# The w_down stage of a hybrid mLSTM and attention block: factor loads on another queue, another order of products, two PSUM banks as one tile

## The chip, the cores and the metric

The kernel runs on one core of a Trainium2 chip. The metric is device time in microseconds (us) of one execution; lower is better. The core's engines work side by side, each through its own list of instructions in order: TensorE (PE in the profile, its weight loads PEld), VectorE (DVE), ScalarE (ACT), GpSimd (POOL) and SyncE (SP). SP, POOL and ScalarE can also start DMA transfers, each from its own queue.

## The reference

One encoder block on x (512 tokens x 2048), all in float32: an RMS norm and input projection, four mLSTM heads and eight differential attention heads, an output projection, and a SwiGLU channel mixer. The change touches only the last product of the mixer:

```python
h2 = rmsnorm(x, norm2_g[l])
x = x + (jax.nn.silu(h2 @ w_gate[l]) * (h2 @ w_up[l])) @ w_down[l]
return rmsnorm(x, final_g)
```

w_down has 5632 rows and 2048 columns.

## The kernel before

Every matmul is done in three: both operands are split into a high part (a ScalarE copy to float32r, L98) and a low part (a VectorE subtraction, L99), and `three` (L157) adds high x high, high x low and low x high. So each operand that comes from memory costs one ScalarE and one VectorE instruction.

The first 4096 rows of w_down are multiplied by Strassen's scheme in Winograd's form, in the loop at L1069. It runs over eight units u: ci, one of four row blocks of 1024, and dg, one of two column halves of 1024. A unit is seven products, P1 to P7, in the order of `DOWN`. A product is 24 matmuls of 512 columns in two PSUM banks (`acc` and `aux`), in two halves h; each half multiplies variants of the activations (left) with one factor of the weights (right).

*Factors.* The generator `left_factors` makes them: per unit and half h, `load` (L885) brings five 512 KB blocks from w_ds on SP's queue: B11 and B22 plainly, T1 and T3 as a plain load and then an accumulating load of a second block on POOL's queue (L891), and B21 plainly. VectorE adds T1 to B22 for P6 (L913) and B21 to it for P4 (L915). `upto` says how many loads the source has asked for at each product. Blocks lie in two rings of seven slots, `raw` (h = 0) and `raw2` (h = 1); `raw2` is opened when the stage before has ended. A factor is split into `whi` and `wlo`, rings of three, and `factor` keeps two more ahead of the one in use, one product.

*Variants.* The activations were written by the stage before to DRAM (`actv`), in seven forms of 256 columns for each row block. `variant` (L946) loads one form in two transfers of 256 KB on SP's queue, into `ra`, a ring of two, and splits each half at once into two tiles of the ring `A`. Both units of a row block use the same seven variants. Those of block 0 are made in the last group of the stage before (four) and in unit 0 (three); those of block ci + 1 in the unit with dg = 1 of block ci, one ahead of each product.

After a product its two banks are copied to `M` by ScalarE (ci = 0, L1088) or added to it by VectorE (L1090), one instruction a bank. After the loop `combine` puts the seven products together, and the other 1536 rows follow in plain products; `last_weights` (L1166) loads and splits the last of their weights while they run.

The order of the instructions on each engine is not that of the source. The framework takes, for each engine, the ready instruction that comes first in the source, by its own model of times; it also sets all waits. On the chip each engine then keeps that order. A tile's slot in a ring is given to the next tile that asks for one once the last reader of the old tile is done.

Of the kernel before, what the change touches and what calls it, by code (L numbers as in the profile page):

```python
# [19 lines left out]
NSP = 4  # L20
# [10 lines left out]
def build(nc, tc, ctx, a, out):  # L31
# [8 lines left out]
    pc = pool("small", 2)  # L40
    pa = pool("pa", 32)
    pW = pool("pw", 3)
    pacc = pool("acc", 4, space=bass.MemoryType.PSUM)
    paux = pool("aux", 4, space=bass.MemoryType.PSUM)
    dram = pool("dr", 1, space=bass.MemoryType.DRAM)

    def stage(*pools):
# [18 lines left out]
        return pT.tile([128, 512], dt, tag="T", name=nm("T"))  # L66

    def tacc():
        return pacc.tile([128, 512], F32, tag="acc", name=nm("acc"))

    def taux():
        return paux.tile([128, 512], F32, tag="aux", name=nm("aux"))

    def tc_(n, p=128, name="c"):
        return cp.tile([p, n], F32, tag=nm("t" + name), name=nm(name))
# [13 lines left out]
    c = {}  # L89
# [752 lines left out]
    def tW(tag, dt=F32, bufs=3):  # L842
        return pW.tile([128, 1024], dt, tag=tag, name=nm(tag), bufs=bufs)

    DOWN = ["P1", "P3", "P6", "P5", "P7", "P4", "P2"]
    more = []

    def tR():
# [2 lines left out]
    def left_factors():  # L851
        def loads(w, g):
            r = []
            for q in range(4):
                t = tW("raw", bufs=7)
                nc.sync.dma_start(t, a[w][g, q])
                r.append(t)
            return r

        def parts(src):  # L860
            hi, lo = tW("whi", F32R), tW("wlo", F32R)
            split(hi, lo, src)
            return hi, lo

        todo = [(w, g) for g in range(NFB) for w in ("w_g", "w_u")]
        nxt = loads(*todo[0])
        for i in range(len(todo)):
            w11, w12, w21, w22 = nxt
            yield parts(w11)
            s1 = tW("raw", bufs=7)  # L870
            V.tensor_tensor(s1, w21, w22, ALU.add)
            V.tensor_tensor(w21, w11, w21, ALU.subtract)
            V.tensor_tensor(w11, s1, w11, ALU.subtract)
            yield parts(w11)
            yield parts(w21)
            yield parts(s1)
            if i + 1 < len(todo):
                nxt = loads(*todo[i + 1])
            yield parts(w12)
            yield parts(w22)  # L880
            V.tensor_tensor(w12, w12, w11, ALU.subtract)
            yield parts(w12)


        def load(u, h, i, ring):  # L885
            j, n, j2, n2 = ((0, 0, 0, 0), (1, 1, 1, 1), (0, 0, 0, 1), (1, 1, 0, 1), (1, 0, 1, 0))[i]
            ci, dg = divmod(u, 2)
            t = ring()
            nc.sync.dma_start(t, a["w_ds"][ci, dg, j, n, h])
            if (j, n) != (j2, n2):  # L890
                G.dma_start(t, a["w_ds"][ci, dg, j2, n2, h], accum_op=ALU.add)  # L891
            return t

        order = [(u, i, h) for u in range(2 * NSP) for i in range(5) for h in range(2)]
        got = {}
        pos = [0]

        def upto(k):
            while pos[0] < min(k, len(order)):
                u, i, h = order[pos[0]]  # L900
                got[u, i, h] = load(u, h, i, tR if h and (u, i) != (0, 0) else lambda: tW("raw", bufs=7))
                pos[0] += 1

        upto(2)
        for u in range(2 * NSP):
            k = 10 * u
            for pi, name in enumerate(DOWN):
                if u or pi:
                    upto(k + (14 if pi == 0 else 16 if pi < 6 else 20))
                for h in range(2):  # L910
                    B11, B22, T1, T3, B21 = (got.get((u, i, h)) for i in range(5))
                    if name == "P6":
                        V.tensor_tensor(B22, B22, T1, ALU.add)  # L913
                    if name == "P4":
                        V.tensor_tensor(B22, B22, B21, ALU.add)  # L915
                    yield parts({"P1": B11, "P3": B22, "P6": B22, "P5": T1, "P7": T3, "P4": B22, "P2": B21}[name])
# [26 lines left out]

    cur_v = {}

    def variant(ci, name, into):  # L946

        v = ["P1", "P7", "P2", "P4", "P5", "P6", "P3"].index(name)
        into[name] = []
        for h in range(2):  # L950
            if more:
                r = more[2].tile([128, 512], F32, tag="ra", name=nm("ra"), bufs=2)
            else:
                r = tW("raw", bufs=7)[:, 0:512]
            g0 = 4 * ci + 2 * h
            nc.sync.dma_start(r.rearrange("p (g c) -> p g c", g=2), actv[g0:g0 + 2, v].rearrange("g p c -> p g c"))
            hi, lo = tA(), tA()
            split(hi, lo, r)
            into[name].append((hi, lo))

    def group(scale, done, first=False, last=False):

        banks = {}
        ps, u, C1, C2 = (tX() for _ in range(4))

        def bank(name):
            if name not in banks:
                banks[name] = (tacc, taux)[len(banks) % 2]()[:, L]
            return banks[name]

        def add(out_, name, other):
            V.tensor_tensor(out_, banks[name], other, ALU.add)

        def after(name):
            if name == "P1":
                SC.copy(ps[:, L], banks[name])
            if name == "P6":
                add(u[:, L], name, ps[:, L])
            if name == "P7":
                add(u[:, R], name, u[:, L])  # L980
            if name == "P5":
                add(C2[:, R], name, u[:, R])
                add(ps[:, R], name, u[:, L])
            if name == "P2":
                add(C1[:, L], name, ps[:, L])
            if name == "P4":
                add(C2[:, L], name, u[:, R])
                done(1, C2)
            if name == "P3":
                add(C1[:, R], name, ps[:, R])  # L990
                done(0, C1)

        order = list(ORDER)
        if first:
            xs = tXS()
            ws = {}
            for i, name in enumerate(order[:3]):
                ws[name] = factor(0)
                product(bank(name), ws[name], name_of(name), range(6))
                if i < 2:  # L1000
                    for j in (2 * i, 2 * i + 1):
                        h2_turn(3, xs, x1, j)
                    for _ in h2_sums(3, xs, slice(i, i + 1)):
                        pass
            for name in order[:3]:
                product(bank(name), ws[name], name_of(name), range(6, 8))
                after(name)
            order = order[3:]
            next(st2)
        for name in order:  # L1010
            w = factor()
            product(bank(name), w, name_of(name))
            if first and name == "P2":
                next(st2)
            after(name)
            if last:
                i = {"P1": 0, "P6": 1, "P5": 2, "P4": 3}.get(name)
                if i is not None:
                    variant(0, DOWN[i], cur_v)

    def name_of(p):
        return RIGHT[p]
# [34 lines left out]
    more.extend(stage(("rr", 1), ("ra", 1)))  # L1057
    more[1:] = more[1]
    M = [{}, {}]

    def product_down(banks, w, name, h):
        for m in range(2):
# [5 lines left out]

    for u in range(2 * NSP):  # L1069
        ci, dg = divmod(u, 2)  # L1070
        got_v = cur_v
        if dg == 1:
            cur_v = {}
        for pi, name in enumerate(DOWN):
            if u == 0 and pi < 3:
                variant(0, DOWN[4 + pi], cur_v)
            if dg == 1 and ci + 1 < NSP:
                variant(ci + 1, name, cur_v)
            banks = [tacc(), taux()]
            for h in range(2):  # L1080
                product_down(banks, factor(), name, h)
            if ci == 0:
                M[dg][name] = pM.tile([128, 1024], F32, tag="M", name=nm("M"), bufs=14)
            t = M[dg][name]
            for tt in range(2):
                cs = slice(tt * 512, tt * 512 + 512)
                if ci == 0:
                    SC.copy(t[:, cs], banks[tt])  # L1088
                else:
                    V.tensor_tensor(t[:, cs], banks[tt], t[:, cs], ALU.add)  # L1090

    more[0].close()
    limit[0] = len(seq)
    last, (pB,) = stage(("fb", 1),)
# [71 lines left out]
    def last_weights():  # L1166

        for b in range(CHUNKS[-1]):
            for n in range(4):
                r = tW("raw", bufs=7)  # L1170
                nc.sync.dma_start(r, a["w_d"][NFB - CHUNKS[-1] + b, n])
                for j in range(2):
                    hi, lo = tL(), tL()
                    split(hi, lo, r[:, j * 512:j * 512 + 512])
                    wL[n][0].append(hi)
                    wL[n][1].append(lo)
                yield

    for ci, nb in enumerate(CHUNKS[:-1]):
        q = chunks[ci]  # L1180
# [55 lines left out]
            nc.sync.dma_start(out[ts, n * 512:n * 512 + 512], xt[n])  # L1236
    last.close()
    mst.close()


def _layout(np, inp):
# [85 lines left out]
```

## Time and profile before

| | |
|---|---|
| time, median of 3 runs | 2180.97 us (2178.7 to 2186.47) |
| profiled execution, its own time | 2190.05 us |
| its span, first to last instruction | 2188.3 us |
| busy | TensorE 2142.0 us (98%), VectorE 1569.6 (72%), ScalarE 992.7 (45%), GpSimd 133.8 (6%) |
| mean granted TensorE clock | 0.991 |
| DMA, whole span | 292.56 MB, mean 134 GB/s |
| the w_down stage, units 0 to 7 | 1693.24 to 2043.60 us |

The profile is of one execution. Times of a row are us from the start of the span; a row's line (L98) is a line of the kernel before. "Idle before, releaser" is the time in which the engine had nothing to do ahead of an instruction, and what ended it. The granted clock is a share of TensorE's full speed; it has two levels, 1.00 (2.4 GHz) and 0.50 (1.2 GHz), and a stretch shows their mean.

### The profile page before, as it was taken

How to read it: one execution, taken by the hardware profiler on the slowest of the kernel's cores; microseconds unless marked ns; L12 is line 12 of the kernel's file. 1: busy time of each engine (PE TensorE's matmuls, PEld its weight loads, DVE VectorE, ACT ScalarE, POOL GpSimd, SP SyncE). 2: the span in 40 equal slices, each digit the busy share in tenths (PEclk: the TensorE clock that was granted, in tenths of full speed). 3: DMA queues.
4: the chain of work that ended last, by engine and by line, in shares of the span. 5: the costliest groups of instructions: out<-in, count | busy, mean ns of one | idle time of the engine just before them, and what ended most of it. 6: DMA issues, size and time to landing. Idle time of an engine off the chain costs nothing.

```text
span 2188.3 us, 33437 instructions
## 1 busy us (share of the span) xinstructions
PE 2142.0 (98%) x13305; PEld 1938.2 (89%) x13305; DVE 1569.6 (72%) x2362; ACT 992.7 (45%) x1515; POOL 133.8 (6%) x189
## 2 busy tenths in 40 slices
PE   9999999999999999999999999999999799999998
PEld 7888889988888889999999999999999577778786
DVE  6267776366544468888888888888889467779745
ACT  6256675355434354344344443343444454444423
POOL 0011110000000000000000000000000000001100
PEclk9999999999999999999999999999999999999999
DMA  6232112332234424343443434433335986876732
GB/s 257 96 96 78 62 53 72 116 97 87 82 112 146 140 92 131 124 145 119 129 135 119 137 121 133 131 123 117 121 121 168 284 228 184 242 210 156 203 106 77
DMA packets 100749, 292.56 MB, mean 134 GB/s; under 512 B 10976, under 2 KB 27376, under 8 KB 100592
## 3 DMA queue, kind: packets, MB, share of 16 engines
q1 hardware_dynamic: 86832, 247.42, 34.5%
q0 software_dynamic: 13760, 43.00, 8.4%
q8 instruction: 104, 1.70, 0.3%
q14 instruction: 53, 0.43, 0.1%
HBM read 264.16 MB, written 26.22 MB: 133 GB/s over the span
## 4 chain that ended last, share of the span: by engine, by line
PE 85%; DMA 6%; DVE 6%; ACT 2%; issue 1%; ACTq 0%; POOL 0%; DVEq 0%; SPq 0%; POOLq 0%
PE acc L159 9%; PE acc L158 9%; PE acc L160 9%; PE acc L933 8%; PE acc L932 8%; PE acc L931 8%; PE aux L933 6%; PE aux L932 6%; PE aux L931 6%; DMA ra<-actv 4%; PE acc L189 4%; PE acc L190 4%; PE acc L191 4%; DVE wlo L99 2%; PE aux L160 1%
## 5 line engine op out<-in xcount | busy, mean ns | idle before, releaser
L98 ACT CAST whi<-raw 128x1024 fp32r<-128x1024 f32 (+2 forms) x573 | 593.6, 1037 | 807.4 <-PE acc L932 238.8
L99 DVE TENSOR_TENSOR wlo<-raw,whi 128x1024 fp32r<-128x1024 f32 (+2 forms) x573 | 690.5, 1206 | 305.8 <-ACT whi L98 295.0
L158 PE MATMUL acc<-whi,A 128*128 128x512 f32 (+1 forms) x1056 | 404.0, 384 | 21.4 <-ACT whi L98 18.2
L159 PE MATMUL acc<-wlo,A 128*128 128x512 f32 (+1 forms) x1056 | 403.7, 382 | 9.5 <-DVE wlo L99 9.5
L160 PE MATMUL acc<-whi,A 128*128 128x512 f32 (+1 forms) x1056 | 400.7, 379 | 0.0
L158 PEld LDWEIGHTS acc<-whi,A 128*128 128x128 f32 x1056 | 200.0, 190 | 59.4 <-ACT whi L98 22.5
L159 PEld LDWEIGHTS acc<-wlo,A 128*128 128x128 f32 x1056 | 200.3, 190 | 48.0 <-DVE wlo L99 15.0
L160 PEld LDWEIGHTS acc<-whi,A 128*128 128x128 f32 x1056 | 200.4, 190 | 34.0
L932 PE MATMUL acc<-A,whi 128*128 128x256 f32 x704 | 199.3, 283 | 0.5 <-DVE A L99 0.5
L931 PE MATMUL acc<-A,whi 128*128 128x256 f32 x704 | 199.4, 283 | 0.0
L931 PE MATMUL acc<-h,whi 128*128 128x256 f32 x704 | 199.4, 283 | 0.0
L933 PE MATMUL acc<-h,wlo 128*128 128x256 f32 x704 | 199.2, 283 | 0.0
L932 PE MATMUL acc<-h,whi 128*128 128x256 f32 x704 | 199.2, 283 | 0.0
L933 PE MATMUL acc<-A,wlo 128*128 128x256 f32 x704 | 199.2, 283 | 0.0
L933 PE MATMUL aux<-h,wlo 128*128 128x256 f32 x528 | 149.7, 284 | 0.8 <-DVE wlo L99 0.8
L931 PE MATMUL aux<-h,whi 128*128 128x256 f32 x528 | 149.6, 283 | 0.6 <-ACT whi L98 0.6
L189 PE MATMUL acc<-A,whi 128*128 128x512 f32 x384 | 150.1, 391 | 0.0
L190 PE MATMUL acc<-A,whi 128*128 128x512 f32 x384 | 149.8, 390 | 0.0
L191 PE MATMUL acc<-A,wlo 128*128 128x512 f32 x384 | 149.8, 390 | 0.0
L933 PE MATMUL aux<-A,wlo 128*128 128x256 f32 x528 | 149.4, 283 | 0.0
L931 PE MATMUL aux<-A,whi 128*128 128x256 f32 x528 | 149.4, 283 | 0.0
L932 PE MATMUL aux<-A,whi 128*128 128x256 f32 x528 | 149.4, 283 | 0.0
(280 smaller groups left out, 4123.9 us busy)
## 6 DMA issues: line engine op xcount, KB each, us to landing
raw<-in_w_g_dram SPq DMA_DIRECT2D x88, 512.0 KB, 3.5
raw<-in_w_u_dram SPq DMA_DIRECT2D x88, 512.0 KB, 3.6
raw<-in_w_ds_dram SPq DMA_DIRECT2D x80, 512.0 KB, 5.1
raw<-in_w_aqk_dram SPq DMA_DIRECT2D x32, 512.0 KB, 3.4
raw<-in_w_o_dram SPq DMA_DIRECT2D x32, 512.0 KB, 3.5
raw<-in_w_ds_dram POOLq DMA_DIRECT2D x32, 512.0 KB, 8.2
raw<-in_w_b_dram SPq DMA_DIRECT2D x31, 512.0 KB, 4.0
actv<-x POOLq DMA_DIRECT2D x48, 256.0 KB, 3.4
```

Source lines behind the costliest of these rows:

```text
L98: SC.copy(hi, src)
L99: V.tensor_tensor(lo, src, hi.bitcast(F32), ALU.subtract)
L158: PE.matmul(acc, lh, rh, start=first, stop=False)
L159: PE.matmul(acc, lh, rl, start=False, stop=False)
L160: PE.matmul(acc, ll, rh, start=False, stop=last)
L189: PE.matmul(banks[f], wh[:, cs], xh[k], start=first, stop=False)
L190: PE.matmul(banks[f], wh[:, cs], xl[k], start=False, stop=False)
L191: PE.matmul(banks[f], wl[:, cs], xh[k], start=False, stop=last)
L931: PE.matmul(bank, w[0][:, cs], hi, start=m == 0, stop=False)
L932: PE.matmul(bank, w[0][:, cs], lo, start=False, stop=False)
L933: PE.matmul(bank, w[1][:, cs], hi, start=False, stop=m == 7)
```

## The change

- The order of the products is P1, P3, P2, P6, P5, P7, P4 (P2 was last), and the blocks of a unit are loaded in the order B11, B22, B21, T1, T3. The last step of `upto` (20 blocks ahead at the last product) is gone; it stays at 16.
- `variant` is divided: `load_v` starts the two transfers, now from ScalarE's queue, and `variant` later splits what was loaded first. In the source the load stands a product before the split. The first variant of block ci + 1 is loaded at product 4 and split at product 6 of the unit with dg = 0; the one used at P1 thus stands a unit before its use, and the others follow from product 1 on in the unit with dg = 1.
- A product's two banks are one PSUM tile of 128x1024, and one instruction copies or adds both. For that the eight single banks are closed before the stage and opened again after it.
- In `last_weights` the step ends between the load and its splits, so that the splits are asked for a step after their load.

```diff
--- before.py
+++ after.py
@@ -40,8 +40,15 @@
     pc = pool("small", 2)
     pa = pool("pa", 32)
     pW = pool("pw", 3)
-    pacc = pool("acc", 4, space=bass.MemoryType.PSUM)
-    paux = pool("aux", 4, space=bass.MemoryType.PSUM)
+    PS = bass.MemoryType.PSUM
+    banks8 = []
+
+    def open_banks():
+        st = ExitStack()
+        banks8[:] = [st] + [st.enter_context(tc.tile_pool(name=n, bufs=4, space=PS, reuse_waits="tile"))
+                            for n in ("acc", "aux")]
+
+    open_banks()
     dram = pool("dr", 1, space=bass.MemoryType.DRAM)
 
     def stage(*pools):
@@ -66,10 +73,10 @@
         return pT.tile([128, 512], dt, tag="T", name=nm("T"))
 
     def tacc():
-        return pacc.tile([128, 512], F32, tag="acc", name=nm("acc"))
+        return banks8[1].tile([128, 512], F32, tag="acc", name=nm("acc"))
 
     def taux():
-        return paux.tile([128, 512], F32, tag="aux", name=nm("aux"))
+        return banks8[2].tile([128, 512], F32, tag="aux", name=nm("aux"))
 
     def tc_(n, p=128, name="c"):
         return cp.tile([p, n], F32, tag=nm("t" + name), name=nm(name))
@@ -842,7 +849,7 @@
     def tW(tag, dt=F32, bufs=3):
         return pW.tile([128, 1024], dt, tag=tag, name=nm(tag), bufs=bufs)
 
-    DOWN = ["P1", "P3", "P6", "P5", "P7", "P4", "P2"]
+    DOWN = ["P1", "P3", "P2", "P6", "P5", "P7", "P4"]
     more = []
 
     def tR():
@@ -883,7 +890,7 @@
 
 
         def load(u, h, i, ring):
-            j, n, j2, n2 = ((0, 0, 0, 0), (1, 1, 1, 1), (0, 0, 0, 1), (1, 1, 0, 1), (1, 0, 1, 0))[i]
+            j, n, j2, n2 = ((0, 0, 0, 0), (1, 1, 1, 1), (1, 0, 1, 0), (0, 0, 0, 1), (1, 1, 0, 1))[i]
             ci, dg = divmod(u, 2)
             t = ring()
             nc.sync.dma_start(t, a["w_ds"][ci, dg, j, n, h])
@@ -906,9 +913,9 @@
             k = 10 * u
             for pi, name in enumerate(DOWN):
                 if u or pi:
-                    upto(k + (14 if pi == 0 else 16 if pi < 6 else 20))
+                    upto(k + (14 if pi == 0 else 16))
                 for h in range(2):
-                    B11, B22, T1, T3, B21 = (got.get((u, i, h)) for i in range(5))
+                    B11, B22, B21, T1, T3 = (got.get((u, i, h)) for i in range(5))
                     if name == "P6":
                         V.tensor_tensor(B22, B22, T1, ALU.add)
                     if name == "P4":
@@ -943,20 +950,26 @@
 
     cur_v = {}
 
-    def variant(ci, name, into):
-
+    loaded = []
+
+    def load_v(ci, name):
         v = ["P1", "P7", "P2", "P4", "P5", "P6", "P3"].index(name)
-        into[name] = []
         for h in range(2):
             if more:
                 r = more[2].tile([128, 512], F32, tag="ra", name=nm("ra"), bufs=2)
             else:
                 r = tW("raw", bufs=7)[:, 0:512]
             g0 = 4 * ci + 2 * h
-            nc.sync.dma_start(r.rearrange("p (g c) -> p g c", g=2), actv[g0:g0 + 2, v].rearrange("g p c -> p g c"))
+            SC.dma_start(r.rearrange("p (g c) -> p g c", g=2), actv[g0:g0 + 2, v].rearrange("g p c -> p g c"))
+            loaded.append((name, r))
+
+    def variant(into):
+
+        for h in range(2):
+            name, r = loaded.pop(0)
             hi, lo = tA(), tA()
             split(hi, lo, r)
-            into[name].append((hi, lo))
+            into.setdefault(name, []).append((hi, lo))
 
     def group(scale, done, first=False, last=False):
 
@@ -1016,7 +1029,9 @@
             if last:
                 i = {"P1": 0, "P6": 1, "P5": 2, "P4": 3}.get(name)
                 if i is not None:
-                    variant(0, DOWN[i], cur_v)
+                    if i:
+                        variant(cur_v)
+                    load_v(0, DOWN[i])
 
     def name_of(p):
         return RIGHT[p]
@@ -1057,6 +1072,9 @@
     more.extend(stage(("rr", 1), ("ra", 1)))
     more[1:] = more[1]
     M = [{}, {}]
+    banks8[0].close()
+    pst = ExitStack()
+    pairs = pst.enter_context(tc.tile_pool(name="pair", bufs=4, space=PS, reuse_waits="tile"))
 
     def product_down(banks, w, name, h):
         for m in range(2):
@@ -1068,27 +1086,37 @@
 
     for u in range(2 * NSP):
         ci, dg = divmod(u, 2)
-        got_v = cur_v
-        if dg == 1:
-            cur_v = {}
+        got_v = cur_v if ci == 0 else nxt_v if dg == 0 else got_v
         for pi, name in enumerate(DOWN):
-            if u == 0 and pi < 3:
-                variant(0, DOWN[4 + pi], cur_v)
-            if dg == 1 and ci + 1 < NSP:
-                variant(ci + 1, name, cur_v)
-            banks = [tacc(), taux()]
+            if u == 0 and pi < 4:
+                variant(cur_v)
+                if pi < 3:
+                    load_v(0, DOWN[4 + pi])
+            if ci + 1 < NSP:
+                if (dg, pi) == (0, 4):
+                    load_v(ci + 1, DOWN[0])
+                if (dg, pi) == (0, 6):
+                    nxt_v = {}
+                    variant(nxt_v)
+                    load_v(ci + 1, DOWN[1])
+                if dg == 1 and pi > 0:
+                    variant(nxt_v)
+                    if pi < 6:
+                        load_v(ci + 1, DOWN[pi + 1])
+            bank = pairs.tile([128, 1024], F32, tag="pair", name=nm("pair"))
+            banks = bank[:, 0:512], bank[:, 512:1024]
             for h in range(2):
                 product_down(banks, factor(), name, h)
             if ci == 0:
                 M[dg][name] = pM.tile([128, 1024], F32, tag="M", name=nm("M"), bufs=14)
             t = M[dg][name]
-            for tt in range(2):
-                cs = slice(tt * 512, tt * 512 + 512)
-                if ci == 0:
-                    SC.copy(t[:, cs], banks[tt])
-                else:
-                    V.tensor_tensor(t[:, cs], banks[tt], t[:, cs], ALU.add)
-
+            if ci == 0:
+                SC.copy(t, bank)
+            else:
+                V.tensor_tensor(t, bank, t, ALU.add)
+
+    pst.close()
+    open_banks()
     more[0].close()
     limit[0] = len(seq)
     last, (pB,) = stage(("fb", 1),)
@@ -1169,12 +1197,12 @@
             for n in range(4):
                 r = tW("raw", bufs=7)
                 nc.sync.dma_start(r, a["w_d"][NFB - CHUNKS[-1] + b, n])
+                yield
                 for j in range(2):
                     hi, lo = tL(), tL()
                     split(hi, lo, r[:, j * 512:j * 512 + 512])
                     wL[n][0].append(hi)
                     wL[n][1].append(lo)
-                yield
 
     for ci, nb in enumerate(CHUNKS[:-1]):
         q = chunks[ci]
@@ -1236,6 +1264,7 @@
             nc.sync.dma_start(out[ts, n * 512:n * 512 + 512], xt[n])
     last.close()
     mst.close()
+    banks8[0].close()
 
 
 def _layout(np, inp):
```

## Rows read from the trace of the kernel before

**Rows 1.** Table by stretch: length, busy us (instructions), granted clock, DMA share, GB/s.

```profile
1693.24:1749.82 56.58, 43.56 (x171) 33.58 (x169) 26.99 (x27) 23.87 (x33) 7.15 (x9) 0.91 0.98 293
1749.82:1795.90 46.08, 42.13 (x169) 33.23 (x168) 29.59 (x31) 28.36 (x42) 3.41 (x4) 0.93 0.81 223
1795.90:1833.98 38.08, 38.08 (x169) 31.53 (x168) 29.71 (x33) 15.78 (x17) 3.40 (x4) 1.00 0.76 213
1833.98:1881.90 47.92, 42.23 (x169) 33.35 (x168) 37.21 (x45) 21.64 (x27) 3.40 (x4) 0.93 0.75 215
...
1919.98:1967.44 47.46, 42.34 (x169) 33.29 (x168) 37.32 (x45) 21.05 (x26) 3.42 (x4) 0.93 0.75 210
...
2005.52:2043.60 38.08, 38.08 (x169) 31.54 (x168) 38.07 (x44) 21.79 (x27) 5.20 (x6) 1.00 0.60 158
2043.60:2135.00 91.40, 88.80 (x385) 73.11 (x384) 47.49 (x57) 30.55 (x42) 6.93 (x8) 0.98 0.49 147
```

**Rows 2.** Timeline of ScalarE and TensorE after the stage: start, us, instruction, [idle, releaser].

```profile
2068.79 1.14 ACT L98 CAST A<-raw 128x512 fp32r<-128x512 f32 x2 [6.53 <-DMA raw<-in_w_d_dram]
...
2070.84 0.77 PE L158 MATMUL acc<-whi,A 128*128 128x512 f32 x1 [2.60 <-DVE M L1186]
```

**Rows 3.** ScalarE's waits, 1690 to 2050: us in total, times, longest.

```profile
ACT A L98 <- DMA ra<-actv: 69.4, 31, 6.2
```

**Rows 4.** Timeline of TensorE in units 0 and 3.

```profile
1714.83 0.80 PE L158 MATMUL acc<-whi,A 128*128 128x512 f32 x1 [5.45 <-ACT whi L98]
...
1872.51 0.50 PE L158 MATMUL acc<-whi,A 128*128 128x512 f32 x1 [2.49 <-ACT whi L98]
```

**Rows 5.** Timeline of VectorE and ScalarE in units 0 and 3.

```profile
1712.42 1.22 DVE L913 TENSOR_TENSOR raw<-raw,raw 128x1024 f32<-128x1024 f32 x1 [6.08 <-DMA raw<-in_w_ds_dram]
...
1713.73 1.04 ACT L98 CAST whi<-raw 128x1024 fp32r<-128x1024 f32 x1 [7.12 <-DVE raw L913]
...
1870.89 0.62 ACT L98 CAST A<-ra 128x512 fp32r<-128x512 f32 x1 [5.50 <-DMA ra<-actv]
```

**Rows 6.** Chain that ended last, units 0 and 3: start, us, what.

```profile
1699.82 19.27 DMA ra<-actv
...
1837.67 0.69 DVE A L99
1838.38 8.56 DMA ra<-actv
...
1861.21 9.65 DMA ra<-actv
```

**Rows 7.** DMA, 1840 to 1843: queue, packets, MB, engine share; issue, us to landing.

```profile
q0 software_dynamic: 126, 0.45, 95.9%
q1 hardware_dynamic: 76, 0.08, 10.3%
...
ra<-actv SPq DMA_DIRECT2D x1, 256.0 KB, 6.3
```

**Rows 8.** Waits of SP's queue, 1690 to 2050.

```profile
SPq L956 <- DVE A L99: 63.9, 44, 4.6
```

**Rows 9.** Timeline of SP's queue in unit 3.

```profile
1861.21 0.38 SPq L956 DMA_DIRECT2D ra<-actv  x1
```

**Rows 10.** VectorE by line and shape, 1795.9 to 2043.6: busy us, mean ns, idle.

```profile
L1090 DVE TENSOR_TENSOR M<-acc,M 128x512 f32<-128x512 f32 x41 | 28.1, 684 | 0.5 <-PE acc L160 0.3
...
L99 DVE TENSOR_TENSOR A<-ra,A 128x512 fp32r<-128x512 f32 x27 | 18.5, 687 | 18.2 <-ACT A L98 17.9
...
L1110 DVE TENSOR_TENSOR M<-M,M 128x1024 f32<-128x1024 f32 x2 | 2.4, 1222 | 0.0
```

**Rows 11.** DMA issues, 1690 to 2045: count, KB each, median us to landing.

```profile
raw<-in_w_ds_dram SPq DMA_DIRECT2D x73, 512.0 KB, 5.0
raw<-in_w_ds_dram POOLq DMA_DIRECT2D x32, 512.0 KB, 8.2
```

## The prediction

> **What bounds the kernel now.** I read the profile in this order: the page (TensorE busy 98%, so only stretches without it count), the table by stretch cut at the units of the w_down stage, the waits, the timeline where TensorE is idle, and the chain for what stood behind.
>
> The table [rows 1] is the main view. A unit is 7 products of 24 matmuls, and each of its rows holds 168 or so. Units 2 and 7 take 38.08 us with TensorE busy throughout at clock 1.00; units 4 and 6 (not shown) take the same to 0.01 us. That is the floor, 5.44 us a product. Units 0, 1, 3 and 5 take 56.58, 46.08, 47.92 and 47.46: lost are 18.5, 8.0, 9.8 and 9.4, together 45.7 us. Only part is idle time (unit 0: 56.58 - 43.56 = 13.0; units 1, 3, 5: 4.0, 5.7, 5.1, being length less busy time). The rest is matmuls at the granted clock of 0.91 to 0.93 that the rows show for the stalled units: it falls to its lower level after a stall. An idle us therefore costs about 1.4 in unit 0 and 1.8 to 2 in the others. In the last row of the table, after the stage, 2.6 us are idle [rows 2] and 0.02 x 91.4 = 1.8 go in clock: 4.4. Everything that this change can win is 45.7 + 4.4 = 50 us.
>
> Who causes it: ScalarE waits 69.4 us for loads into `ra`, the factors of the variants [rows 3]. It works in order, so the next `whi` copy stands behind the wait, and TensorE waits for that copy [rows 4]. The reader sees it in the pair 1870.89 (ScalarE, 5.50 idle for `ra`) [rows 5] and 1872.51 (TensorE, 2.49 idle for `whi`) [rows 4]. The run-ahead of the factors swallows the first 3 us. In unit 0 there is another cause: at P6, VectorE's add of T1 waits until 1712.42 for the accumulating DMA, ScalarE 7.12 for that add, TensorE 5.45 for ScalarE [rows 4, 5].
>
> Why `ra` is late [rows 6]: 19.27 us at 1699.82, 8.56 at 1838.38, 9.65 at 1861.21. The first stands behind the w_ds loads on SP's queue while the DMA engines are 0.98 busy [rows 1]. The second shares the engines with accumulating DMAs. In 1840 to 1843 [rows 7] POOL's queue moved 126 packets and held 95.9% of the engines' time, SP's 76: a 4 KB accumulating packet costs 0.959 x 48 / 126 = 0.37 us of an engine (16 engines x 3 us = 48), and the short packets of `ra` (1 KB each by the kernel) pass not far from one for one with them. A half of a variant is 256 packets, 16 an engine: 16 x (0.37 + 0.05) = 6.7 us, and that issue took 6.3.
>
> **Plain blocks first.** Nothing is added or removed: ten loads and four accumulates a unit. In unit 0, P6's second half was due at 1693.24 + 2.5 x 5.44 = 1706.8 and began at 1714.83, 8.0 late. Now it is due a product later, at 1712.3. T1 stands one 512 KB load further back, 0.524 MB at 293 GB/s [rows 1] = 1.8 us, so it arrives at 1714.2, and the add and the copy take the 2.4 us that they took (1712.42 to 1714.83): 1716.6, 4.3 late. Gain 3.7, with its share of the clock 5.3. Bounds: 0 (T1 back by a full product, if its accumulate loses DMA time to `ra`) and all 8.0 x 1.4 = 11.
>
> In the later units the order changes when the accumulates run. A load goes out when a slot is free, not when the source line is reached: 1837.67 + 0.69 ends the split that frees `ra`, and the load follows at 1838.38 [rows 6]. Before, T1 of the next unit takes the slot of B11 at P1, and T3 that of T1 at P5's split: two short accumulating stretches, each with a late `ra`. After, T1 and T3 take the slots of B21 and T1 with the splits for P6 and P5: all four accumulates in one stretch, none in the first three products.
>
> **Variants on ScalarE's queue, a product ahead.** By the same row, `ra` was already requested when its slot came free, so "a product ahead" moves little. What moves is the queue. SP's queue waited 63.9 us for `ra` slots [rows 8], with w_ds loads held up behind; that goes, and `ra` no longer stands behind w_ds loads. ScalarE pays 56 issues at about 0.38 us [rows 9], 21 us over the stage, hidden: it is busy 21.64 of 47.92 us in unit 3 [rows 1]. An issue also waits for VectorE's split (0.69 us each [rows 10]); queued behind it on ScalarE is the next `whi`, for which TensorE waits only when it is later than the run-ahead of 3 us. Without that cover two issues would cost 0.76 + 1.4 = 2.2 us.
>
> The Trainium skill (DMA: Bandwidth & Descriptors, Issuing engines are not separate DMA queues) speaks against this part: transfers started from several engines run on the same 16 DMA engines, and only issue time is saved. By that rule this edit gives nothing, and without its 3.2 and the 11 below the sum would be 6 us. The trace half agrees: SP's and POOL's packets do share [rows 7], but the issue held up on SP was 63.9 us.
>
> Price in units 1, 3 and 5 (27.2 lost): the two late transfers in unit 3 are about equal (8.56, 9.65), so with the first stretch about half goes, 13.6; the stretch that is left is twice as long, so I take 11. Bounds 0 and 27.2. In unit 0 the idle time other than at P6, 13.0 - 5.45 = 7.6, is 10.8 with clock; those are `ra` waits under engines still 0.98 busy. I take 3.2; bounds 0 and 10.8.
>
> **Two banks as one tile.** Two additions of 0.684 become one, nearest the 1.222 of a 128x1024 addition [rows 10]; the pair now waits for the last matmul. VectorE is busy 37.2 of 47.9 in unit 3 [rows 1] and 38.07 of 38.08 in unit 7, without a stall there: nothing, bounds -1 and +3. Changing PSUM pools at either end of the stage may hold the first product for the last 128x256 addition of the stage before (below 1 us each): I take +1 together.
>
> **First factor split a unit ahead** takes 2 x 0.69 us of VectorE from the stalled units to the quiet ones; it is in the 11. **The last weights' split a step later** lets ScalarE pass the wait of 6.53 us that ends in the 2.60 idle [rows 2]: between 0 and 4.4, I take 2.
>
> **Sum.** 5.3 + 3.2 + 11 + 2 - 1 = 20.5 us off the profiled execution (span 2188.3, its own time 2190.05). The median is 2180.97, 9 lower than that execution, so I take the 20.5 off the median: 2160.5, say 2160.
>
> **Rivals.**
> *All of it goes.* `ra` on its own queue lands before ScalarE needs it. For: the 69.4 us is by far the longest DMA wait, and units 2 and 4 run clean at DMA shares of 0.76 to 0.78 [rows 1], no lower than the 0.75 of units 3 and 5. Against: P6 of unit 0 stays 4.3 late, about 6 with the clock. 50 - 6 = 44 off: 2137.
>
> *The edit does not do what it says.* `ra` was already asked for as soon as its slot was free [rows 6], the bytes are the same and the engines are shared, so the waits change place only: one longer accumulating stretch costs in units 1, 3 and 5 what two short ones did. Left are P6 of unit 0, the tail and the pools, 5.3 + 2 - 1 = 6: 2175. For: the 0.98 of unit 0 and the packets in 1840 to 1843 [rows 7]. Against: in units 2 and 4 the same w_ds transfers hide completely. This is also what the Trainium skill's rule above makes of it.
>
> *Slower: `ra` is starved in the long accumulating stretch.* With three queues taking turns, a packet of `ra` passes per round of one accumulating packet (0.37), one plain (0.18: a 4 KB plain packet at half that cost is an estimate from 8.2 against 5.0 us to landing and the double work [rows 11]) and itself: 16 x 0.6 = 9.6 us a half, 19 for both, where SP's queue took 8.6 to 9.7 a half but started the halves apart. ScalarE then stands about 10 us longer in each of units 0, 1, 3 and 5, less 3 of run-ahead, 7 each: +28, less the 5.3 of P6: 2204. It decides once a half takes longer than about 10 us on the new queue. For: four accumulates make 32 packets an engine, all in one stretch. Against: with SP free its loads are over sooner, and then a round is 0.42.
>
> **Chances.** Forecast (part goes, -8 to -34) 0.44; all goes 0.24; nothing changes 0.14; starved 0.18. By sign, with 0.3% (6.5 us, about what this kernel's measurement can tell) as the bound: faster 0.68, same 0.14, slower 0.18. The range goes from a little beyond the second case, 2133, to just past no change, 2186, which leaves out most of the starved case and little else; the forecast's own range is 2147 to 2173.
>
> **What would show it.** In the table by units of the new trace: units 2, 4, 6, 7 at 38.1 still; unit 0 near 46 to 48; units 1, 3, 5 near 43 to 44 with the loss in their last three products; no TensorE idle time near 2070. ScalarE's waits for `ra` fall from 69 to about 40 us, and SP's waits for `ra` slots are gone. Wrong would be: a unit other than these stalls (T1 or T3, now loaded closer to their use, late at P6 or P7); ScalarE idle behind its own DMA issues; VectorE holding the `whi` chain.

## The result and the profile after

The change makes the kernel slower: 2207.04 us (2203.59 to 2210.54, 4 runs) against 2183.3 for the kernel before in the same runs, a ratio of 1.011 (95% interval 1.0083 to 1.0138). The forecast was 2160. The rival that was given 0.18, "`ra` is starved in the long accumulating stretch", had 2204.

The same table as [rows 1], for the changed kernel, cut at the first matmul of each unit (length, then busy us and instructions of TensorE, its weight loads, VectorE, ScalarE and GpSimd, granted clock, DMA share, GB/s):

```profile
1695.52:1751.94 56.42, 44.62 (x169) 35.21 (x170) 25.98 (x25) 22.30 (x25) 6.88 (x9) 0.85 0.87 252
1751.94:1805.12 53.18, 41.00 (x169) 33.07 (x168) 28.93 (x30) 28.05 (x34) 3.40 (x4) 0.87 0.78 228
1805.12:1843.20 38.08, 38.08 (x169) 31.54 (x168) 29.60 (x26) 16.25 (x16) 3.40 (x4) 1.00 0.68 190
1843.20:1893.96 50.76, 41.59 (x169) 32.97 (x168) 36.58 (x37) 21.71 (x27) 3.40 (x4) 0.90 0.75 217
1893.96:1932.04 38.08, 38.08 (x169) 31.54 (x168) 30.73 (x27) 15.40 (x15) 3.39 (x4) 1.00 0.66 194
1932.04:1980.10 48.06, 41.00 (x170) 32.53 (x168) 33.32 (x34) 20.13 (x26) 3.43 (x4) 0.93 0.74 213
1980.10:2025.28 45.18, 40.56 (x170) 32.51 (x168) 36.02 (x33) 17.66 (x20) 5.14 (x6) 0.96 0.61 159
2025.28:2063.98 38.70, 38.70 (x170) 31.31 (x169) 38.70 (x38) 22.57 (x28) 6.95 (x8) 1.00 0.63 159
2063.98:2208.77 144.79, 131.49 (x577) 107.69 (x575) 77.26 (x118) 48.40 (x85) 5.21 (x6) 0.98 0.39 120
```

Row by row against before, in the two profiled executions: the stage starts 2.3 us later, unit 0 is 0.2 shorter, unit 1 is 7.1 longer, unit 3 2.8, unit 5 0.6, unit 6 (which lost nothing) 7.1, unit 7 0.6, and what follows the stage 0.1. That is the whole 20.5 us between the spans of 2208.8 and 2188.3.

In unit 1 the timeline (start, us, instruction, idle time and its releaser) shows why: ScalarE first, then TensorE.

```profile
1788.44 0.62 ACT L105 CAST A<-ra 128x512 fp32r<-128x512 f32 x1 [10.77 <-DMA ra<-actv]
...
1794.84 0.62 ACT L105 CAST A<-ra 128x512 fp32r<-128x512 f32 x1 [4.87 <-DMA ra<-actv]
1795.36 1.04 ACT L105 CAST whi<-raw 128x1024 fp32r<-128x1024 f32 x1
...
1796.45 0.80 PE L165 MATMUL pair<-whi,A 128*128 128x512 f32 x1 [11.72 <-ACT whi L105]
```

ScalarE stands 10.8 and 4.9 us for two halves of one variant, with the next `whi` behind them. The chain (start, us, what) has the second of these loads at 17.06 us from issue, where the slow ones of before took 8.6 and 9.7 [rows 6]:

```profile
1777.75 17.06 DMA ra<-actv
```

GpSimd's timeline shows what those loads met. All four accumulating loads of the unit start within 9 us; before, in unit 3, they started at 1835.12, 1837.85, 1858.18 and 1859.52.

```profile
1775.04 0.84 POOL L898 DMA_DIRECT2D raw<-in_w_ds_dram  x1 [31.00 <-ACT M L1114]
1779.44 0.84 POOL L898 DMA_DIRECT2D raw<-in_w_ds_dram  x1 [3.56 <-DVE wlo L106]
1780.74 0.85 POOL L898 DMA_DIRECT2D raw<-in_w_ds_dram  x1 [0.46 <-issue]
1783.74 0.86 POOL L898 DMA_DIRECT2D raw<-in_w_ds_dram  x1 [2.15 <-DMA raw<-in_w_ds_dram]
```

The DMA view of 1776 to 1795 (queue, packets, MB, share of 16 engines) has the three queues side by side; q0 is GpSimd's, q1 SP's, q10 ScalarE's:

```profile
q0 software_dynamic: 575, 2.10, 55.9%
q1 hardware_dynamic: 548, 1.97, 31.1%
q10 hardware_dynamic: 785, 0.76, 12.3%
```

Over the 19 us ScalarE's queue moved 1.4 packets for each one of the others, but its packets are a quarter of their size: 0.76 MB. In 1782 to 1789, while two of its loads were under way beside the others, the three took turns one for one:

```profile
q0 software_dynamic: 236, 0.84, 59.9%
q1 hardware_dynamic: 243, 0.92, 34.9%
q10 hardware_dynamic: 244, 0.24, 10.2%
```

Unit 3 shows a second way in which the new queue delays `ra`. A load can go out when VectorE's split has freed its slot. One slot was free at 1866.68 + 0.68 = 1867.36, but the issue stands in ScalarE's order behind a split that waits for the load before, and went out at 1872.54, 5.2 us later; its own data then held ScalarE for 9.56 us. VectorE first, then ScalarE and its queue:

```profile
1866.68 0.68 DVE L106 TENSOR_TENSOR A<-ra,A 128x512 fp32r<-128x512 f32 x1
...
1872.53 0.62 ACT L105 CAST A<-ra 128x512 fp32r<-128x512 f32 x1 [6.31 <-DMA ra<-actv]
1872.54 0.37 ACTq L963 DMA_DIRECT2D ra<-actv  x1
1883.66 0.62 ACT L105 CAST A<-ra 128x512 fp32r<-128x512 f32 x1 [9.56 <-DMA ra<-actv]
```

In the same way loads went out 4.7 us late in unit 0 and 3.7 and 3.2 in unit 5. In unit 1 the loads of the stall went out within 0.2 us of their slots, so there late issues are not the reason.

Unit 0 loses its time at its start. ScalarE's split of a variant now stands ahead of the second `whi` of P3, and waits:

```profile
1701.56 0.62 ACT L105 CAST A<-ra 128x512 fp32r<-128x512 f32 x1 [6.73 <-DMA ra<-actv]
1707.51 0.62 ACT L105 CAST A<-ra 128x512 fp32r<-128x512 f32 x1 [5.32 <-DMA ra<-actv]
...
1719.07 0.62 ACT L105 CAST A<-ra 128x512 fp32r<-128x512 f32 x1 [9.94 <-DMA ra<-actv]
```

Unit 6, which loads no variant, is stopped by another load that ScalarE has to split, for the products after the stage, under the same four accumulates (10.78 us from issue by the chain):

```profile
2018.98 1.14 ACT L105 CAST A<-raw 128x512 fp32r<-128x512 f32 x2 [6.72 <-DMA raw<-actd]
```

And the first product of the stage waits for the last addition of the stage before, as its bank pair is not free:

```profile
1695.52 0.47 PE L165 MATMUL pair<-whi,A 128*128 128x512 f32 x1 [1.82 <-DVE x L985]
```

In total ScalarE waited 84.3 us for `ra` (before 69.4 [rows 3]), in 22 waits instead of 31.

### The profile page after: what moved, and what is told of

Its sections match the earlier page's. It is cut to its first block, busy times and chain, and to the rows that moved or that the text cites. A ratio compares the mean times of both kernels' runs of the same rounds, so it can differ in the third digit from the quotient of the medians.

```text
span 2208.8 us, 33345 instructions
## 1 busy us (share of the span) xinstructions
PE 2142.5 (97%) x13305; PEld 1938.3 (88%) x13305; DVE 1565.9 (71%) x2320; ACT 991.4 (45%) x1501; POOL 133.9 (6%) x189
## 4 chain that ended last, share of the span: by engine, by line
PE 87%; DMA 5%; DVE 5%; ACT 2%; issue 1%; ACTq 0%; POOL 0%; DVEq 0%; POOLq 0%
PE acc L165 8%; PE acc L166 8%; PE acc L167 8%; PE acc L940 7%; PE acc L939 7%; PE acc L938 7%; PE aux L940 6%; PE aux L939 6%; PE aux L938 6%; DMA ra<-actv 4%; PE acc L196 3%; PE acc L197 3%; PE acc L198 3%; PE pair L166 3%; PE pair L167 3%; PE pair L165 3%
## 5 line engine op out<-in xcount | busy, mean ns | idle before, releaser
L165 PE MATMUL acc<-whi,A 128*128 128x512 f32 (+1 forms) x832 | 313.3, 378 | 4.3 <-DVE M L1214 2.2
L166 PE MATMUL acc<-wlo,A 128*128 128x512 f32 (+1 forms) x832 | 311.3, 374 | 0.0
L167 PE MATMUL acc<-whi,A 128*128 128x512 f32 (+1 forms) x832 | 310.7, 373 | 0.0
L165 PE MATMUL pair<-whi,A 128*128 128x512 f32 x448 | 180.7, 403 | 40.0 <-ACT whi L105 38.2
L166 PE MATMUL pair<-wlo,A 128*128 128x512 f32 x448 | 181.5, 405 | 6.6 <-DVE wlo L106 6.6
L165 PEld LDWEIGHTS acc<-whi,A 128*128 128x128 f32 x832 | 156.7, 188 | 30.4 <-DVE M L1214 2.6
L167 PE MATMUL pair<-whi,A 128*128 128x512 f32 x448 | 178.9, 399 | 0.0
L167 PEld LDWEIGHTS acc<-whi,A 128*128 128x128 f32 x832 | 156.2, 188 | 25.4
L166 PEld LDWEIGHTS acc<-wlo,A 128*128 128x128 f32 x832 | 156.3, 188 | 24.4 <-DVE wlo L106 0.5
```

What stands on the lines that cost most here:

```text
L165: PE.matmul(acc, lh, rh, start=first, stop=False)
L166: PE.matmul(acc, lh, rl, start=False, stop=False)
L167: PE.matmul(acc, ll, rh, start=False, stop=last)
```

## The experiments

The theory: two edits together do the harm. The new order puts a unit's four accumulates into one stretch, and the new queue makes `ra` the third party there, with small packets. Rivals: the queue alone, the order alone, or (for the mechanism) DMA engines that are simply full. Each ratio is to the kernel before in the same runs. Tables by unit are of one profiled execution each. In the expectations e3 is the changed kernel with SP's queue, and e12 the version whose additions are on GpSimd.

**The order alone**, in the kernel before:

```diff
-    DOWN = ["P1", "P3", "P6", "P5", "P7", "P4", "P2"]
+    DOWN = ["P1", "P3", "P2", "P6", "P5", "P7", "P4"]
...
-                    upto(k + (14 if pi == 0 else 16 if pi < 6 else 20))
+                    upto(k + (14 if pi == 0 else 16))
```

(and the blocks loaded as B11, B22, B21, T1, T3).

> The kernel before with the new order of products and blocks alone; variants on SP's queue. Theory (the four accumulates of a unit in one stretch, and the 1 KB packets of ra on a third queue, starve ra together): the long stretch is there, but ra stands in SP's queue, where it takes turns with the accumulates alone, so units 1, 3 and 5 lose about as before, 27 us, unit 0 a few less at P6: 2175 to 2190. Rival, the order alone does it: units 1, 3, 5 lose 35 to 38 and unit 6 loses 7: 2195 to 2207. Rival, the queue alone does it: no loss beyond before, 2170 to 2183.

2188.9 us, ratio 1.0023 (1.0008 to 1.0037). Units 3, 4, 5 and 6 of its table:

```profile
1833.91:1875.85 41.94, 39.03 (x170) 31.20 (x168) 33.54 (x42) 19.30 (x24) 3.40 (x4) 1.00 0.80 241
1875.85:1917.28 41.43, 39.45 (x168) 31.40 (x169) 33.89 (x38) 17.26 (x18) 3.40 (x4) 1.00 0.68 191
1917.28:1959.45 42.17, 38.24 (x169) 31.34 (x167) 33.59 (x42) 19.30 (x24) 3.43 (x4) 1.00 0.82 251
1959.45:2007.64 48.19, 42.72 (x168) 34.24 (x169) 39.25 (x42) 19.62 (x22) 6.85 (x8) 0.90 0.66 162
```

With SP's queue the order does what was forecast of it: units 3 and 5 lose 3.9 and 4.1 where they lost 9.8 and 9.4 [rows 1], though unit 1 loses 0.8 more. But units 4 and 6 lose 3.3 and 10.1, unit 6 to the load for the products after the stage (ScalarE waits 8.60 us for it). Units 1, 3 and 5 lose 16.8 us together, where I had expected 27, and units 4 and 6 give the gain back; the total is even or a little worse. The order alone is not the cause.

**The queue alone**, in the kernel before:

```diff
-            nc.sync.dma_start(r.rearrange("p (g c) -> p g c", g=2), ...
+            SC.dma_start(r.rearrange("p (g c) -> p g c", g=2), ...
```

> The kernel before with the variants' loads on ScalarE's queue alone; old order. Theory: the accumulates stay in two short stretches, SP is freed of its waits for ra slots, ra takes turns with three queues: units 1, 3, 5 lose 20 to 30, 2170 to 2190. Rival, the queue alone does it: 2195 to 2207, with ra landing 13 to 17 us after its issue in units 1, 3, 5. Rival, the order alone: 2165 to 2183, unit 6 without loss.

2189.49 us, 1.0022 (1.0006 to 1.0037). Units 1, 3 and 5 take 45.6, 46.7 and 47.0, 0.5 to 1.2 less than before; units 2 and 4 take 1.9 and 1.0 more. SP is rid of its waits for `ra` and waits elsewhere:

```profile
SPq L889 <- DVE wlo L99: 252.5, 65, 17.3
```

The row of the kernel before:

```profile
SPq L889 <- DVE wlo L99: 141.4, 65, 13.6
```

Before, SP waited 141.4 us for the slots of w_ds blocks and 63.9 for those of `ra` [rows 8]; now it waits 252.5 for w_ds slots alone. Its time was not what held the loads up. The queue alone is not the cause either.

**The changed kernel less one of the two.** First the variants back on SP's queue, then the old order of products and blocks, all else as changed.

> The changed kernel with the variants' loads back on SP's queue, all else kept. Theory: the two waits of 10.8 and 4.9 us in unit 1 shrink to at most 6 each, 2180 to 2192; what is left above before is the pools (2.3) and unit 6 (7). Rival, the order alone: as the changed kernel, 2203 to 2210. Rival, the queue alone: at or below before, 2170 to 2183.

> The changed kernel with the old order of products and blocks, all else kept (variants on ScalarE's queue, split a product later, banks as one tile). Theory: the accumulates fall into two short stretches again, unit 6 loses nothing, units 1, 3, 5 lose 20 to 28: 2178 to 2192. Rival, the queue alone: 2203 to 2210. Rival, the order alone: 2170 to 2185.

2189.32 us, 1.0019 (1.0004 to 1.0034), and 2192.61 us, 1.0041 (1.0026 to 1.0056), the second 0.6 us above its range. Taking away either edit removes most of the loss:

| ratio to before | variants on SP's queue | variants on ScalarE's queue |
|---|---|---|
| old order, rest as before | 1 | 1.0022 |
| new order, rest as before | 1.0023 | not run |
| old order, rest as changed | not run | 1.0041 |
| new order, rest as changed | 1.0019 | 1.0110 |

Most of the harm needs both edits. By units, putting `ra` back on SP's queue takes 22.2 us off units 1, 3 and 5 and 3.4 off unit 0, and units 2 and 4 give 6.0 back. The loss of unit 6 comes with the order, on either queue (10.1 in the order alone, 7.7 with SP's queue, 7.1 in the changed kernel); with the old order unit 6 takes 38.08 on either. On SP's queue, in the kernel before and in the changed one, no `ra` load of units 1 to 7 goes out more than 0.2 us after its slot is free. With the queue alone some go out up to 7.4 us late, and that costs 0.2%, so late issues alone are not the harm. Nor are long landings alone: in the changed kernel with SP's queue single loads still take 12.0, 13.9 and 14.8 us by the chain, in units 1, 3 and 5. There unit 1's accumulates start over 15.7 us, from 1768.87 to 1784.61, instead of 8.7. So three things come with the new queue, a third party in the turns, late issues and closer accumulates, and these runs do not separate them. Nor is it shown that the pair would do the same harm without the earlier load and the single tile, as that was not run.

**Larger packets.** `actv` is laid out so that the two groups of a half lie side by side, and a half is read in 2 KB packets, 8 an engine instead of 16. Bytes, order and queue are the same. In the changed kernel, in the kernel before, and in the changed kernel with SP's queue:

```diff
-    actv = dram.tile([4 * NSP, 7, 128, 256], F32, name="actv")
+    actv = dram.tile([2 * NSP, 7, 128, 2, 256], F32, name="actv")
...
-            SC.dma_start(r.rearrange("p (g c) -> p g c", g=2), actv[g0:g0 + 2, v].rearrange("g p c -> p g c"))
+            SC.dma_start(r, actv[g0 // 2, v].rearrange("p g c -> p (g c)"))
```

> The changed kernel with actv laid out so that a half of a variant is read in 2 KB packets, 8 an engine where it was 16; same bytes, queue and order. Theory (ra gets about one packet a turn, so the number of its packets sets its time while the accumulates run): the halves that landed 13 and 17 us after issue in unit 1 land in 7 to 10, ScalarE's waits for ra fall from 84 to 40 to 50 us, units 1, 3, 5 lose 20 instead of 38: 2180 to 2192. Rival (the engines are simply full, ra waits for bytes): no change, 2203 to 2210.

> The kernel before with the same 2 KB packets. Theory: ra under accumulates (8.6 and 9.7 us in unit 3) lands in 5 to 6, ScalarE's waits for ra fall from 69 to 40 to 50, 15 us off: 2165 to 2175. Rival (bytes): within 6 us of before.

> The changed kernel with the variants back on SP's queue and read in 2 KB packets. Theory: as e3 with ra's share of the loss about halved, 2165 to 2178; unit 6 keeps its 7. Rival (bytes): as e3, 2186 to 2192.

In the changed kernel: 2198.55 us, 1.0059 (1.0044 to 1.0074); 8.5 us came off the median, and the ratio fell from 1.0110. In 1782 to 1785, in unit 1, with all three queues at work:

```profile
q0 software_dynamic: 95, 0.32, 54.1%
q1 hardware_dynamic: 98, 0.40, 34.9%
q10 hardware_dynamic: 92, 0.18, 15.3%
```

The turns are still about one for one, and each now carries 2 KB for `ra`. The load that took 17.06 us takes 10.15 by the chain, and unit 1 takes 46.3 instead of 53.2. Full engines alone would have shown no change, so in the changed kernel that rival falls; but the time that was expected (2180 to 2192) was missed by 7 us, unit 5 gained nothing (48.2), and ScalarE still waits 74.3 us for `ra`. In the kernel before: 2179.37 us, 0.9982 (0.9972 to 0.9992), faster, by a quarter to a third of the 15 us that were expected and within the 6 us of the rival. With SP's queue and the new order: 2188.05 us, 1.0013 (1.0003 to 1.0022), little or no better than with 1 KB packets, in the rival's range and against the expectation: units 4 and 6 still lose 4.8 and 10.3. So the size of its packets matters where `ra` has a queue of its own; on SP's queue these runs do not show that it is what holds `ra` up.

**No accumulates**, in the changed kernel. T1 and T3 are left as one block each, so four of the seven factors (P6, P5, P7, P4) lack a block; the instructions and all other loads are as before.

```diff
-            if (j, n) != (j2, n2):
+            if False:
                 G.dma_start(t, a["w_ds"][ci, dg, j2, n2, h], accum_op=ALU.add)
```

> The changed kernel without the 32 accumulating loads (T1 and T3 are one block each, so the factors of five of the seven products are not the scheme's); all else kept. Theory: ra has only SP's 4 KB packets to take turns with, a half lands in 3 to 5 us, units 1 to 7 lose under 3 us each, unit 0 5 to 10: 2145 to 2160. Rival (ScalarE's own issues and waits, or VectorE's load, hold the factors): units 1, 3, 5 keep half of their loss or more, 2180 or above.

2163.76 us, 0.9896 (0.9877 to 0.9914), 4 above the range that was expected. Units 1 to 7 lose at most 1.3 us each; unit 1 is now

```profile
1744.58:1782.98 38.40, 38.39 (x169) 31.45 (x168) 28.36 (x30) 27.47 (x33) 0.00 (x0) 1.00 0.63 199
```

and unit 0 keeps 11.8. With ScalarE's queue, its issues and its waits for VectorE all in place, the loss in units 1, 3, 5 and 6 is gone: without the accumulates neither the turns nor the late issues cost it. Which part of an accumulate does it, its bytes, its slow packets or its waits, this run does not say.

**Two banks as one tile, with the pools**, alone in the kernel before.

> The kernel before with the two banks of a product as one tile, and the PSUM pools changed at both ends of the stage, alone. Theory: the first product of the stage starts 2 us later (it waits for the last addition of the stage before), VectorE and ScalarE gain nothing: +1 to +4, 2185 to 2189. Rival (the tile delays the additions and with them the factors): units 2, 4, 6, 7 no longer run at 38.1, +10 or more.

2183.7 us, 1.0001 (0.9986 to 1.0015). It costs and brings nothing that these runs can tell; the stage starts 1.4 us later, and units 1, 2, 4 and 6 are within 1.1 us of before.

**A version without accumulates.** T1 = B11 + W and T3 = B22 + W share the block W, and B11 and B22 are on the chip already. So W is loaded once, plainly, and added: T1 in the slot of B11, T3 in that of W. A unit loads 8 blocks instead of 10 and 4 accumulates. Old order, SP's queue, 2 KB packets; the additions on GpSimd, on GpSimd with T1's on VectorE in units with dg = 0, or all on VectorE. The number of blocks that are asked for ahead (`upto`) is set anew for 8 blocks a unit. The last of the three, cut:

```diff
-            j, n, j2, n2 = ((0, 0, 0, 0), (1, 1, 1, 1), (0, 0, 0, 1), (1, 1, 0, 1), (1, 0, 1, 0))[i]
+            j, n = ((0, 0), (1, 1), (0, 1), (1, 0))[i]
...
+                if pi == 1:
+                    for h in range(2):
+                        B11, B22, W12 = (got[u, i, h] for i in range(3))
+                        V.tensor_tensor(B11, B11, W12, ALU.add)
+                        V.tensor_tensor(W12, W12, B22, ALU.add)
```

> The kernel before with 2 KB packets for the variants and no accumulating loads: T1 and T3 share a block, which is loaded once and added on GpSimd to B11 and to B22, so 8 blocks a unit instead of 10 and 4 accumulates; old order, SP's queue. Theory (the accumulates are what holds ra up): ra lands in 3 to 5 us, units 1 to 7 lose under 3 us each, unit 0 5 to 12: 2150 to 2165. Rival: GpSimd's additions are late for P6, or slow VectorE while both run: 2180 or above, with TensorE waiting at P6 of every unit.

> As e12, with T1's additions on VectorE in the units with dg = 0. Theory: as e12, within 6 us. Rival (GpSimd late): better than e12 in units 0, 2, 4, 6 alone.

> As e12, with all four additions of a unit on VectorE: 4 x 1.22 = 4.9 us more in units where it is busy 37.2 (dg = 1) and 38.07 (unit 7) of 38.1. Theory: those units lose 4 us each, 2165 to 2180. Rival (GpSimd is the problem, VectorE is not full): 2150 to 2165.

On GpSimd 2190.02 us, 1.0029 (1.0018 to 1.0041); mixed 2182.8, 0.9996 (0.9981 to 1.001); on VectorE 2163.96, 0.991 (0.9883 to 0.9936). The last beats both kernels: 20 us under the one before, and 43 under the changed one by their medians. The 2 KB packets alone gave 4 to 5 of the 20. In its table unit 0 takes 39.8 us instead of 56.6; ScalarE waits 18.9 us for `ra`. Its rival held: VectorE is not full, and the units with dg = 1 lose 0 to 2.0 us. What is left lies mostly in units 4 and 6, 5.9 and 5.6 (ScalarE waits 40.0 us over the stage for VectorE's addition for P6):

```profile
1733.44:1771.52 38.08, 38.08 (x170) 31.54 (x168) 32.29 (x34) 28.08 (x42) 0.00 (x0) 1.00 0.60 194
...
1849.98:1893.97 43.99, 40.29 (x169) 32.56 (x168) 37.88 (x42) 16.20 (x17) 0.00 (x0) 0.96 0.39 123
```

On GpSimd the rival held: an addition takes 2.8 to 3.0 us there, and every unit takes 43 to 46 us. Mixed, the rival held too: units 0, 2, 4 and 6 are 1.0 to 3.6 us shorter than with GpSimd alone, the others within 0.6.

## Why the prediction was wrong

**What bounds the kernel** was read rightly: ScalarE standing in order for `ra`, with accumulates as the reason. Without accumulates even the changed kernel runs 21 us under the kernel before.

**"Plain blocks first"** was forecast to put all four accumulates in one stretch, and it does (four starts within 9 us). That half of the losses in units 1, 3 and 5 would go with the first stretch holds on SP's queue: 6.0 and 5.3 off units 3 and 5 in the order alone and 0.8 more in unit 1, together 10.4 of the 11; in the changed kernel with SP's queue it is 11.6. So there the 11 was about the right size. What was missed, a term put at nothing: any load that ScalarE splits is caught in the long stretch. Units 4 and 6 had been counted as quiet; in the order alone they lose 3.3 and 10.1, and in the changed kernel unit 6 loses 7.1, to a load for the products after the stage.

**"Variants on ScalarE's queue"** is the step that failed. It was priced at 11 (with the order) and 3.2 in unit 0, on the ground that SP's 63.9 us of waits for `ra` slots held w_ds loads up. Measured: units 1, 3 and 5 together 10.5 us longer than before, unit 0 even; against the changed kernel with SP's queue 22.2 and 3.4 longer, and 18 us in the median. SP had time to spare (252.5 us of waits for w_ds slots when `ra` is gone from its queue). The rule of the Trainium skill that was weighed against this part (DMA: Bandwidth & Descriptors, Issuing engines are not separate DMA queues) was nearer than the row that I set against it: alone, the edit gave nothing (1.0022). Together with the order it cost. On SP's queue `ra` takes turns with the accumulates alone [rows 7]; on its own it takes turns with SP's packets too, though how much of the cost that is stays open. And the prediction asked what stands behind an issue on ScalarE, the next `whi`, but not what stands before it: a split that waits for the load before, which held issues back by 3.2 to 5.2 us.

**The starved rival** had the turns right and the total (2204), the total in part by luck. Its price of a half, 9.6 us, compares with 13.45 and 17.06 in unit 1 (the first by its issue at 1774.99 and the split at 1788.44); its price of both, 19, with 19.8 from the first issue to 1777.75 + 17.06. It was given 0.18 because with SP free "its loads are over sooner"; they were not: the median from issue to landing of the w_ds loads on SP's queue is 7.1 us where it was 5.0 [rows 11]. Its place was partly wrong: of the 28 us, units 1, 3 and 5 gave 10.5 and unit 0 nothing, and unit 6 and the start of the stage, of which it said nothing, made up 9.4.

**P6 of unit 0**: the 5.3 us did not come, because P3 stalled first, on ScalarE's order. On SP's queue unit 0 was 1.4 us shorter in the order alone and 3.6 in the changed kernel.

**Two banks as one tile**: nothing, as said; the stage starts 2.3 us later in the changed kernel and 1.4 alone, against 1 forecast for both ends. How much of that is the pools is open: the wait for the bank pair is 1.82, but with the queue alone, without the tile, the stage starts 2.7 later.

**The last weights' split**: 2 forecast, 0.1 lost. What follows the stage takes 144.8 us against 144.7; TensorE's one wait of 2.6 has become two, of 1.6 and 2.2.

Left open: why the changed kernel with 2 KB packets is still 10 us slower than with SP's queue and the same packets, and how much of the 0.2% that each edit costs alone is real, as it is near what the runs can tell.

## What to carry to other kernels

A load that a strictly ordered engine will wait for must not meet a long run of heavy packets: look up, before a transfer is moved or an order is changed, what else is in flight at that time, in packets and not only in bytes. A queue that waits for slots is not a queue that is short of time; moving its transfers to another queue bought nothing here and made one more party that takes turns, and on the queue of an engine that works in order a load waits behind that engine's own waits. When accumulating transfers are what holds the others up, ask if the sum can be made on the chip from blocks that are there already: here that saved 6 of a unit's 14 transfers and, with the larger packets, 20 us, of which the packets alone gave 4 to 5.

## What the runs showed of the hardware

While three queues had packets waiting they took turns close to one for one, whatever the size: 244 to 243 to 236 with 1 KB packets on ScalarE's queue, 92 to 98 to 95 with 2 KB (the counts show the shares, not the order on an engine). In 1776 to 1795 of the changed kernel an accumulating 4 KB packet held an engine for 0.559 x 16 x 19 us / 575 = 0.30 us, a plain one of SP's queue for 0.311 x 304 / 548 = 0.17, one of `ra` for 0.123 x 304 / 785 = 0.05, all with the short packets counted in. The prediction had 0.37, 0.18 and 0.05.

An addition of 128x1024 on GpSimd takes 2.8 to 3.0 us and slows VectorE, here by line (busy us, mean ns), first GpSimd's, then VectorE's in the same kernel:

```profile
L912 POOL TENSOR_TENSOR raw<-raw,raw 128x1024 f32<-128x1024 f32 x16 | 48.2, 3015 | 1.2
L911 POOL TENSOR_TENSOR raw<-raw,raw 128x1024 f32<-128x1024 f32 x16 | 44.7, 2794 | 233.5 <-DVE wlo L99 233.4
```

```profile
L99 DVE TENSOR_TENSOR A<-ra,A 128x512 fp32r<-128x512 f32 x26 | 26.4, 1015 | 3.0 <-ACT A L98 3.0
L1093 DVE TENSOR_TENSOR M<-acc,M 128x512 f32<-128x512 f32 x38 | 25.9, 682 | 0.0
...
L916 DVE TENSOR_TENSOR raw<-raw,raw 128x1024 f32<-128x1024 f32 x10 | 20.3, 2034 | 0.3
```

The subtraction from `ra` takes 1015 ns there and 687 before [rows 10], the addition 2034 against 1220 with everything on VectorE; the addition out of PSUM stays at 682. One pair of this addition shows it: the first runs while GpSimd adds, from 1827.57 to 1834.28, and the second after it.

```profile
1828.81 3.24 DVE L916 TENSOR_TENSOR raw<-raw,raw 128x1024 f32<-128x1024 f32 x1
...
1838.82 1.21 DVE L916 TENSOR_TENSOR raw<-raw,raw 128x1024 f32<-128x1024 f32 x1
```

The Trainium skill (SBUF — State Buffer, Terms) says that VectorE and GpSimd hold a shared pair of ports by an exclusive lock, the loser blocked; these rows agree for operands in SBUF. The 32 additions on GpSimd cost more than the accumulates they replaced: 1.0029, against 0.9982 with the 2 KB packets alone.
